# Gate and up products of the experts over 512 columns, and the next expert's transposes placed after the down products

## The chip, the cores and the metric

The kernel runs on one core of a Trainium2 chip. The metric is the time of one execution on the device in microseconds; the figure of the kernel before is the median of its runs, and a profiled execution stands beside them.

## What is computed

The kernel is one layer of an encoder: two token mixers over 2048 tokens of 1024 channels, then a mixture of 16 experts. The change touches the experts alone. Each expert takes the 256 tokens that score highest for it, and adds its weighted output to them:

```python
cap = CAPACITY_FACTOR * T // N_EXPERTS          # 256
top_vals, top_idx = lax.top_k(jnp.swapaxes(affinity, 1, 2), cap)
xs = h[b_idx, top_idx]
hid = jax.nn.silu(jnp.einsum('becd,edf->becf', xs, w_gate)) * jnp.einsum('becd,edf->becf', xs, w_up)
ys = jnp.einsum('becf,efd->becd', hid, w_down) * top_vals[..., None].astype(h.dtype)
return jnp.zeros_like(h).at[b_idx, top_idx].add(ys)
```

## The kernel before, in words

Every number goes into TensorE as two parts of type float32r: a high part (a copy that rounds) and a low part (what the rounding left). A product of two matrices is then three products on TensorE, written in `mm3` (L89 to L93): high weights by high tokens, high weights by low tokens, low weights by high tokens, all into one sum in PSUM. `split` (L96) makes the two parts: a copy on ScalarE (L97) and a subtraction on VectorE (L98).

`stage4` (L1192) walks through 128 parts, n = 0 to 127: 16 experts (e) by 8 blocks (f) of 128 hidden channels. For part n the loop writes, in this order: the splitting of the weights of part n+1 (`weights`, L1256: gate and up together as `wg`, down as `wd`), the load of the raw weights of part n+3 (1.5 MB, on SyncE's queue), the gate and up products of part n (L1330 to L1334: gate, then up, each 8 inner blocks by three products of 256 columns, both into one PSUM tile `pg`), SiLU of the gate on ScalarE (L1336), its product with up on VectorE (L1337), the split of the result into `hd` (L1339), and then the down products of part n-1 (`down`, L1263: 12 products of 512 columns into the four PSUM tiles `py`). So a part is 48 products of 256 columns and 12 of 512 on TensorE.

Beside this, for the next expert: at f = 1 `slots` (L1210) finds the token numbers with 32 small products and issues two gathers of tokens on GpSimd's queue; at f = 3 and f = 4 `turn` (L1241) turns each gathered block `x` of 128 tokens into the layout `xs` of the products. It does so in two halves: four transposes on TensorE into a PSUM tile `pt4`, a copy to the high part on ScalarE (L1248), a subtraction to the low part on VectorE (L1249). The first expert's tokens are turned ahead of the loop (L1315). At f = 0 of the next expert, `result` (L1269) adds the finished `py` tiles to the rows of the output.

The eight PSUM banks of this stage: two for `pt4` (shared by `slots` and `turn`), two for `pg`, four for `py`.

The order in which each engine gets its instructions isn't the order of the text alone. A planner walks through the program with a simulated clock and gives each engine the earliest instruction in the text that is ready by that clock. The order is then fixed, and each engine works it off in turn. `tc.issue_after(ins)` makes the planner place a block's instructions for that engine behind `ins`.

Of the kernel before, what the change touches and what calls it, by code (L numbers as in the profile page):

```python
# [9 lines left out]
F32 = mybir.dt.float32  # L10
F32R = mybir.dt.float32r
BF16 = mybir.dt.bfloat16
I32 = mybir.dt.int32
AF = mybir.ActivationFunctionType
ALU = mybir.AluOpType
AX = mybir.AxisListType
PSUM = bass.MemoryType.PSUM
# [3 lines left out]
KD = D // 128  # L21
# [12 lines left out]
CAP = 2 * T // NEXP  # L34
# [26 lines left out]
def pool(tc, **kw):  # L61

    return tc.tile_pool(reuse_waits="tile", **kw)
# [25 lines left out]
def mm3(nc, out, w, x, start=True, stop=True):  # L89

    nc.tensor.matmul(out, lhsT=w[0], rhs=x[0], start=start, stop=False)  # L91
    nc.tensor.matmul(out, lhsT=w[0], rhs=x[1], start=False, stop=False)  # L92
    return nc.tensor.matmul(out, lhsT=w[1], rhs=x[0], start=False, stop=stop)  # L93


def split(nc, hi, lo, x, eng=None):  # L96
    nc.scalar.activation(hi, x, AF.Copy)  # L97
    (eng or nc.vector).tensor_sub(lo, x, hi)  # L98
# [1093 lines left out]
def stage4(k, out):  # L1192


    nc, tc = k.nc, k.tc
    with ExitStack() as es:
# [4 lines left out]
        xt = es.enter_context(pool(tc, name="xtp", bufs=2))  # L1201
        wr = es.enter_context(pool(tc, name="wr4", bufs=3))
        ws = es.enter_context(pool(tc, name="ws4", bufs=3))
        hp = es.enter_context(pool(tc, name="hp", bufs=2))
# [5 lines left out]
        def slots(e):  # L1210

            ps = ps_t.tile([128, 2, 5], F32, name="pt4")
            for t in range(NBLK):
                o = oh.tile([128, CAP], BF16, name="o")
                nc.vector.tensor_scalar(o, k.iota, k.pos[:, t, e:e + 1], None, op0=ALU.is_equal)
                for h in range(2):
                    nc.tensor.matmul(ps[:, h], lhsT=o[:, h * 128:h * 128 + 128], rhs=k.r5[:, t, e],
                                     start=(t == 0 and h == 0), stop=(t == NBLK - 1), skip_group_check=True)
            g = ip.tile([128, 2, 5], F32, name="g")
            nc.vector.tensor_copy(g, ps)  # L1220
            idx = ip.tile([128, 2], I32, name="idx")
            nc.vector.scalar_tensor_tensor(out=idx, in0=g[:, :, 0], scalar=128.0, in1=g[:, :, 1],
                                           op0=ALU.mult, op1=ALU.add)
            tv = ip.tile([128, 2], F32, name="tv")
            nc.vector.tensor_add(tv, g[:, :, 2], g[:, :, 3])
            nc.vector.tensor_add(tv, tv, g[:, :, 4])
            x = []
            for h in range(2):
                x.append(xg.tile([128, D], F32, name="x"))
                gather(x[h], k.h2, idx[:, h:h + 1])  # L1230
            return idx, tv, x

        def gather(dst, src, idx):
            nc.gpsimd.indirect_dma_start(out=dst, out_offset=None, in_=src,
                                         in_offset=bass.IndirectOffsetOnAxis(ap=idx, axis=0))
# [2 lines left out]
            nc.gpsimd.indirect_dma_start(out=dst, out_offset=bass.IndirectOffsetOnAxis(ap=idx, axis=0),  # L1238
                                         in_=src, in_offset=None)

        def turn(x, xs, h):  # L1241

            for half in range(2):
                pt = ps_t.tile([128, 4, 128], F32, name="pt4")
                for i in range(4):
                    nc.tensor.transpose(pt[:, i], x[h][:, (half * 4 + i) * 128:(half * 4 + i + 1) * 128], k.ident)
                sl = (slice(None), slice(half * 4, half * 4 + 4), slice(h * 128, h * 128 + 128))
                nc.scalar.activation(xs[:, 0][sl], pt, AF.Copy)  # L1248
                nc.vector.tensor_sub(xs[:, 1][sl], pt, xs[:, 0][sl])  # L1249

        def load(n):
            raw = wr.tile([128, 3, KD, 128], F32, name="raw")
            nc.sync.dma_start(raw, k.I["w_exp"][n // KD, n % KD])
            return raw

        def weights(raw, eng=None):  # L1256
            wg = ws.tile([128, 2, 2, KD, 128], F32R, name="wg")
            split(nc, wg[:, 0], wg[:, 1], raw[:, 0:2], eng)
            wd = ws.tile([128, 2, KD * 128], F32R, name="wd")
            split(nc, wd[:, 0], wd[:, 1], raw[:, 2].rearrange("p a b -> p (a b)"), eng)  # L1260
            return wg, wd

        def down(e, f, hd, wd, py):  # L1263
            for h in range(2):
                for n in range(2):
                    mm3(nc, py[h * 2 + n], [hd[:, s, h * 128:h * 128 + 128] for s in range(2)],
                        [wd[:, s, n * 512:n * 512 + 512] for s in range(2)], start=(f == 0), stop=(f == KD - 1))

        def result(py, idx, tv, z, last):  # L1269
            for h in range(2):  # L1270
                ss = fp.tile([128, 1], F32, name="ssf")
                for n in range(2):
                    sl = slice(n * 512, n * 512 + 512)
                    nc.vector.scalar_tensor_tensor(out=z[h][:, sl], in0=py[h * 2 + n], scalar=tv[:, h:h + 1],
                                                   in1=z[h][:, sl], op0=ALU.mult, op1=ALU.add)
                if not last:
                    scatter(k.x2, z[h], idx[:, h:h + 1])
                o = yp.tile([128, D], F32, name="o")
                nc.scalar.activation(o, z[h], AF.Square, accum_out=ss)
                nc.vector.tensor_scalar(ss, ss, 1.0 / D, EPS, op0=ALU.mult, op1=ALU.add)  # L1280
                rs = fp.tile([128, 1], F32, name="rsf")
                rsqrt(k, fp, rs, ss)
                nc.vector.scalar_tensor_tensor(out=o, in0=z[h], scalar=rs, in1=gf, op0=ALU.mult, op1=ALU.mult)
                scatter(out, o, idx[:, h:h + 1])
# [22 lines left out]
        raws = [load(i) for i in range(3, 6)]  # L1307
        small = pieces([x for t in lo for x in t])
        route(k, rp, small)
        ps_t = es.enter_context(pool(tc, name="ps_t4", bufs=2, space=PSUM))  # L1310
        ps_g = es.enter_context(pool(tc, name="ps_g", bufs=2, space=PSUM))
        ps_y = es.enter_context(pool(tc, name="ps_y4", bufs=4, space=PSUM))
        nxt = slots(0)
        xs_n = xt.tile([128, 2, KD, CAP], F32R, name="xs")
        for h in range(2):  # L1315
            turn(nxt[2], xs_n, h)
# [3 lines left out]
        for n in range(N + 1):  # L1320
            e, f = divmod(n, KD)
            if n < N:
                if f == 0:
                    (idx, tv, _), xs = nxt, xs_n
                if 2 < n + 1 < N:
                    w.append(weights(raws.pop(0)))
                if 5 < n + 3 < N:
                    raws.append(load(n + 3))
                wg, wd = w.pop(0)
                pg = ps_g.tile([128, 2, CAP], F32, name="pg")  # L1330
                for a in range(2):
                    for i in range(KD):
                        mm3(nc, pg[:, a], [wg[:, s, a, i] for s in range(2)], [xs[:, s, i] for s in range(2)],
                            start=(i == 0), stop=(i == KD - 1))  # L1334
                sg = hp.tile([128, CAP], F32, name="sg")
                nc.scalar.activation(sg, pg[:, 0], AF.Silu)  # L1336
                nc.vector.tensor_mul(sg, pg[:, 1], sg)  # L1337
                hd = hp.tile([128, 2, CAP], F32R, name="hd")
                split(nc, hd[:, 0], hd[:, 1], sg)  # L1339
            if prev is not None:  # L1340
                pe, pf, phd, pwd, ppy, pidx, ptv = prev
                down(pe, pf, phd, pwd, ppy)
                if pf == KD - 1:
                    result(ppy, pidx, ptv, z, pe + 1 == NEXP)
            if n == N:
                break
            if f == 0:
                py = [ps_y.tile([128, 512], F32, name="py") for _ in range(4)]
            prev = (e, f, hd, wd, py, idx, tv)
            if e + 1 < NEXP:  # L1350
                if f == 1:
                    nxt = slots(e + 1)
                elif f == 3:
                    xs_n = xt.tile([128, 2, KD, CAP], F32R, name="xs")
                    turn(nxt[2], xs_n, 0)
                elif f == 4:
                    turn(nxt[2], xs_n, 1)
            if f == 5:
                z = [yp.tile([128, D], F32, name="z") for _ in range(2)]
                for h in range(2):  # L1360
                    gather(z[h], k.x2, idx[:, h:h + 1])
# [37 lines left out]
def build(tc, I, out, stop=None, mk=None):  # L1399
    k = K()  # L1400
    k.tc, k.nc, k.I, k.stop = tc, tc.nc, I, stop
    with ExitStack() as es:
# [30 lines left out]
        if stop == "stage3":  # L1433
            return
        stage4(k, out)


# [105 lines left out]
```

## Time and profile before

| | us |
|---|---|
| median of 3 runs | 3432.81 |
| lowest, highest | 3432.05, 3434.65 |
| the profiled execution's own time | 3430.81 |
| its span, first to last instruction | 3429.0 |
| stage 4's products, first to last | 2275.4 to 3413.8 of the span |

The times are of the device. The rows in the section below come from the profiled execution; their times are microseconds from its span's start, and L91 is line 91 of the kernel. "PEld" is the load of weights into TensorE, which runs beside a product. A product's row has a modelled end that overlaps the next one's start, so the pace is read from start to start.

### The profile page before, as it was taken

Reading aid. Unit: us, or ns where it says so; the run is one execution under the profiler, and the core shown is the slowest. Engines: PE = TensorE matmul, PEld = TensorE weight load, DVE = VectorE, ACT = ScalarE, POOL = GpSimd, SP = SyncE. Lnnn points to the kernel's source line nnn. Section 1 sums busy time; section 2 is a strip of 40 time slices with the busy share of each in tenths; the row PEclk is TensorE's granted clock in tenths of the full one; section 3 lists DMA queues with packets and bytes.
Section 4 is the critical chain, followed back from the end, with each engine's and each line's share of the span. In section 5 each row is a group of like instructions: output and inputs, shape, how many; then the busy total and the mean of one; then the engine's idle time right before and its main releaser. Section 6 shows DMA issues by size and latency. Waiting matters only on the chain. (4 is left out here: it accounts for less than half of the span.)

```text
span 3429.0 us, 65646 instructions
## 1 busy us (share of the span) xinstructions
PE 3175.8 (93%) x26062; PEld 2609.1 (76%) x26062; DVE 2321.8 (68%) x4902; ACT 1469.0 (43%) x2828; POOL 286.5 (8%) x457
## 2 busy tenths in 40 slices
PE   7999898889879988999979999769999999999998
PEld 6888777667656655666647888559999999999997
DVE  6434679798868889666776666466666666666665
ACT  5111455545434545455553333314444444444443
POOL 0000000000021111001000000001112111121111
PEclk9999999899989998999989999879999999999999
DMA  4222687878787777577656554336666666666663
GB/s 146 83 74 89 186 251 218 244 209 244 217 205 186 166 186 171 141 195 177 178 180 229 197 197 166 147 122 241 218 237 237 245 243 225 230 245 244 236 233 124
DMA packets 464579, 665.19 MB, mean 194 GB/s; under 512 B 162312, under 2 KB 345480, under 8 KB 445968
## 3 DMA queue, kind: packets, MB, share of 16 engines
q1 hardware_dynamic: 387824, 535.14, 50.5%
q10 hardware_dynamic: 58304, 59.79, 5.4%
q0 software_dynamic: 18144, 66.07, 5.1%
q8 instruction: 206, 3.38, 0.4%
q14 instruction: 101, 0.83, 0.1%
HBM read 483.66 MB, written 177.21 MB: 193 GB/s over the span
## 5 line engine op out<-in xcount | busy, mean ns | idle before, releaser
L500 PE MATMUL mm<-h,w 128*128 128x512 f32 x2112 | 604.6, 420 | 26.9 <-ACT ev L524 7.7
L91 PE MATMUL pg<-xs,wg 128*128 128x256 f32 x2048 | 583.7, 285 | 0.0
L92 PE MATMUL pg<-xs,wg 128*128 128x256 f32 x2048 | 582.1, 284 | 0.0
L93 PE MATMUL pg<-xs,wg 128*128 128x256 f32 x2048 | 579.6, 283 | 0.0
L500 PEld LDWEIGHTS mm<-h,w 128*128 128x128 f32 x2112 | 385.7, 195 | 121.2 <-DVE h L98 10.2
L92 PEld LDWEIGHTS pg<-xs,wg 128*128 128x128 f32 x2048 | 392.5, 192 | 4.6 <-DVE xs L1249 0.2
L91 PEld LDWEIGHTS pg<-xs,wg 128*128 128x128 f32 x2048 | 392.3, 192 | 4.6 <-ACT xs L1248 0.2
L93 PEld LDWEIGHTS pg<-xs,wg 128*128 128x128 f32 x2048 | 392.4, 192 | 0.0
L98 DVE TENSOR_TENSOR wg<-raw,wg 128x2048 fp32r<-128x2048 f32 x125 | 286.2, 2290 | 106.0 <-ACT wg L97 105.8
L97 ACT ACTIVATE w<-wraw 128x1024 fp32r<-128x1024 f32 x135 | 142.6, 1058 | 302.5 <-issue 155.1
L1336 ACT ACTIVATE sg<-pg 128x256 f32<-128x256 f32 x128 | 49.3, 385 | 488.2 <-PE pg L93 459.8
L97 ACT ACTIVATE wg<-raw 128x2048 fp32r<-128x2048 f32 x125 | 238.5, 1908 | 0.0
L410 DVE TENSOR_TENSOR tmp<-X,N 128x1 f32<-128x1 f32 (+30 forms) x248 | 188.7, 761 | 40.4 <-DMA N<-pra 26.9
L83 PE MATMUL mm<-h,w 128*128 128x512 f32 x480 | 190.0, 396 | 20.5 <-ACT w L97 12.8
L92 PE MATMUL py<-wd,hd 128*128 128x512 f32 x512 | 203.1, 397 | 0.0
L671 ACT ACTIVATE W<-ps 32x128 f32<-32x128 f32 x512 | 137.1, 268 | 150.0 <-PE ps L666 128.6
L91 PE MATMUL py<-wd,hd 128*128 128x512 f32 x512 | 201.0, 393 | 0.0
L93 PE MATMUL py<-wd,hd 128*128 128x512 f32 x512 | 198.4, 390 | 0.0
L98 DVE TENSOR_TENSOR w<-wraw,w 128x1024 fp32r<-128x1024 f32 x135 | 164.9, 1223 | 47.6 <-ACT w L97 47.2
L84 PE MATMUL mm<-h,w 128*128 128x512 f32 x480 | 188.8, 394 | 0.0
L85 PE MATMUL mm<-h,w 128*128 128x512 f32 x480 | 188.6, 393 | 0.0
L1337 DVE TENSOR_TENSOR sg<-pg,sg 128x256 f32<-128x256 f32 x128 | 54.1, 423 | 192.9 <-ACT sg L1336 192.9
(302 smaller groups left out, 6385.9 us busy)
## 6 DMA issues: line engine op xcount, KB each, us to landing
raw<-w_exp SPq DMA_DIRECT2D x128, 1536.0 KB, 7.7
wraw<-w_in SPq DMA_DIRECT2D x103, 512.0 KB, 4.3
PRA<-pra SPq DMA_DIRECT2D x64, 512.0 KB, 4.7
pra<-PR SPq DMA_DIRECT2D x64, 256.0 KB, 4.3
pra<-A SPq DMA_DIRECT2D x64, 256.0 KB, 3.9
kt<-KT ACTq DMA_DIRECT2D x128, 128.0 KB, 5.0
gl<-ev ACTq DMA_DIRECT2D x64, 256.0 KB, 4.0
KT<-kt SPq DMA_DIRECT2D x128, 128.0 KB, 4.6
```

The lines of the kernel that those rows point to most:

```text
L83: nc.tensor.matmul(ps, lhsT=w[:, 0, i], rhs=hs[i][:, 0], start=(i == 0), stop=False)
L84: nc.tensor.matmul(ps, lhsT=w[:, 0, i], rhs=hs[i][:, 1], start=False, stop=False)
L85: nc.tensor.matmul(ps, lhsT=w[:, 1, i], rhs=hs[i][:, 0], start=False, stop=(i == KD - 1))
L91: nc.tensor.matmul(out, lhsT=w[0], rhs=x[0], start=start, stop=False)
L92: nc.tensor.matmul(out, lhsT=w[0], rhs=x[1], start=False, stop=False)
L93: return nc.tensor.matmul(out, lhsT=w[1], rhs=x[0], start=False, stop=stop)
L97: nc.scalar.activation(hi, x, AF.Copy)
L98: (eng or nc.vector).tensor_sub(lo, x, hi)
L410: nc.vector.tensor_mul(tmp[:, :i, :i], X[:, r, r], col[:, None, :].to_broadcast([128, i, i]))
L500: nc.tensor.matmul(self.ps, lhsT=w[:, t // 2, i], rhs=h[:, t % 2], start=(self.i == 0), stop=(self.i == 3 * KD - 1))
L671: nc.scalar.activation(W[qd(u), o, e].rearrange("p g i -> p (g i)"), ps[qd(u), 128:256], AF.Copy)
L1337: nc.vector.tensor_mul(sg, pg[:, 1], sg)
```

## The change

`mm3` is no longer used for gate and up. Its first two products, which have the same weights, become one product of 512 columns: the high weights by both parts of the tokens (`xs[:, :, i]`, two runs of 256), with the high part's sum in the first 256 columns of a PSUM tile and the low part's in the last 256. The third product, low weights by high tokens, goes on into the first 256 columns. So gate and up each fill a PSUM tile of their own, and the two halves of it are added afterwards: ScalarE copies one half out, VectorE adds the other. `ps_g` has three banks in place of two, and `ps_t` one in place of two.

The next expert's transposes come as one half in each of the parts f = 4, 5, 6 and 7, placed behind the last down product that the same part issues.

```diff
-        def turn(x, xs, h):
+        def turn(x, xs, h, halves=(0, 1)):
-            for half in range(2):
+            for half in halves:
                 pt = ps_t.tile([128, 4, 128], F32, name="pt4")
...
         def down(e, f, hd, wd, py):
             for h in range(2):
                 for n in range(2):
-                    mm3(nc, py[h * 2 + n], [hd[:, s, h * 128:h * 128 + 128] for s in range(2)],
+                    mm = mm3(nc, py[h * 2 + n], [hd[:, s, h * 128:h * 128 + 128] for s in range(2)],
                         [wd[:, s, n * 512:n * 512 + 512] for s in range(2)], start=(f == 0), stop=(f == KD - 1))
+            return mm.ins
...
-        ps_t = es.enter_context(pool(tc, name="ps_t4", bufs=2, space=PSUM))
-        ps_g = es.enter_context(pool(tc, name="ps_g", bufs=2, space=PSUM))
+        ps_t = es.enter_context(pool(tc, name="ps_t4", bufs=1, space=PSUM))
+        ps_g = es.enter_context(pool(tc, name="ps_g", bufs=3, space=PSUM))
...
-                pg = ps_g.tile([128, 2, CAP], F32, name="pg")
+                gu = []
                 for a in range(2):
+                    pg = ps_g.tile([128, 2, CAP], F32, name="pg")
                     for i in range(KD):
-                        mm3(nc, pg[:, a], [wg[:, s, a, i] for s in range(2)], [xs[:, s, i] for s in range(2)],
-                            start=(i == 0), stop=(i == KD - 1))
-                sg = hp.tile([128, CAP], F32, name="sg")
-                nc.scalar.activation(sg, pg[:, 0], AF.Silu)
-                nc.vector.tensor_mul(sg, pg[:, 1], sg)
+                        nc.tensor.matmul(pg, lhsT=wg[:, 0, a, i], rhs=xs[:, :, i], start=(i == 0), stop=False)
+                        nc.tensor.matmul(pg[:, 0], lhsT=wg[:, 1, a, i], rhs=xs[:, 0, i], start=False,
+                                         stop=(i == KD - 1))
+                    t = hp.tile([128, CAP], F32, name=f"gu{a}")
+                    nc.scalar.activation(t, pg[:, 1], AF.Copy)
+                    nc.vector.tensor_add(t, pg[:, 0], t)
+                    gu.append(t)
+                    if a == 0:
+                        nc.scalar.activation(t, t, AF.Silu)
+                sg = gu[0]
+                nc.vector.tensor_mul(sg, gu[1], sg)
...
-                down(pe, pf, phd, pwd, ppy)
+                last = down(pe, pf, phd, pwd, ppy)
...
-                elif f == 3:
-                    xs_n = xt.tile([128, 2, KD, CAP], F32R, name="xs")
-                    turn(nxt[2], xs_n, 0)
-                elif f == 4:
-                    turn(nxt[2], xs_n, 1)
+                elif f >= 4:
+                    if f == 4:
+                        xs_n = xt.tile([128, 2, KD, CAP], F32R, name="xs")
+                    with tc.issue_after(last):
+                        turn(nxt[2], xs_n, (f - 4) // 2, (f % 2,))
```

## Rows read from the trace of the kernel before

**Rows 1.** The page's first part: busy time, share of the span, instructions.

```profile
PE 3175.8 (93%) x26062; PEld 2609.1 (76%) x26062; DVE 2321.8 (68%) x4902; ACT 1469.0 (43%) x2828; POOL 286.5 (8%) x457
```

**Rows 2.** Windows: one stretch, its length, busy time of each engine, clock, DMA.

```profile
2400.00:3400.00 1000.00, 1000.00 (x7405) 936.57 (x7404) 650.34 (x1209) 456.07 (x561) 162.37 (x110) 1.00 0.64 232
```

**Rows 3.** Timeline of PE, one part: start, length, engine, line, operation, tiles.

```profile
2700.13 0.40 PE L91 MATMUL py<-wd,hd 128*128 128x512 f32 x1
2700.36 0.40 PE L92 MATMUL py<-wd,hd 128*128 128x512 f32 x1
2700.60 0.39 PE L93 MATMUL py<-wd,hd 128*128 128x512 f32 x1
...
2702.88 0.28 PE L91 MATMUL pg<-xs,wg 128*128 128x256 f32 x1
2702.99 0.28 PE L92 MATMUL pg<-xs,wg 128*128 128x256 f32 x1
...
2703.35 0.28 PE L92 MATMUL pg<-xs,wg 128*128 128x256 f32 x1
...
2708.63 0.40 PE L91 MATMUL py<-wd,hd 128*128 128x512 f32 x1
```

**Rows 4.** Timeline of ACT over the end of a part, idle time and releaser in brackets.

```profile
2407.30 0.39 ACT L1336 ACTIVATE sg<-pg 128x256 f32<-128x256 f32 x1 [4.08 <-PE pg L93]
2407.58 1.91 ACT L97 ACTIVATE wg<-raw 128x2048 fp32r<-128x2048 f32 x1
2409.38 0.40 ACT L97 ACTIVATE hd<-sg 128x256 fp32r<-128x256 f32 x1
2409.99 1.06 ACT L97 ACTIVATE wd<-raw 128x1024 fp32r<-128x1024 f32 x1 [0.20 <-PE py L93]
```

**Rows 5.** Timeline of DVE over the same stretch.

```profile
2407.72 0.42 DVE L1337 TENSOR_TENSOR sg<-pg,sg 128x256 f32<-128x256 f32 x1 [2.58 <-ACT sg L1336]
2409.52 2.29 DVE L98 TENSOR_TENSOR wg<-raw,wg 128x2048 fp32r<-128x2048 f32 x1 [1.38 <-ACT wg L97]
2411.73 0.42 DVE L98 TENSOR_TENSOR hd<-sg,hd 128x256 fp32r<-128x256 f32 x1
2412.06 1.22 DVE L98 TENSOR_TENSOR wd<-raw,wd 128x1024 fp32r<-128x1024 f32 x1
```

**Rows 6.** Timeline of all engines where one block of tokens is turned.

```profile
2396.22 1.04 PE L1246 MATMUL pt<-ident,x 128*128 128x128 f32 x8
2396.86 1.09 ACT L1248 ACTIVATE xs<-pt 128x512 fp32r<-128x512 f32 x2 [4.53 <-PE pt L1246]
...
2397.02 0.36 PE L92 MATMUL pg<-xs,wg 128*128 128x256 f32 x1
...
2397.22 0.28 PE L93 MATMUL pg<-xs,wg 128*128 128x256 f32 x1
```

**Rows 7.** Timeline of all engines ahead of the first part.

```profile
2271.08 1.97 PE L1246 MATMUL pt<-ident,x 128*128 128x128 f32 x8 [5.86 <-DMA x<-h,idx]
2272.23 0.60 ACT L1248 ACTIVATE xs<-pt 128x512 fp32r<-128x512 f32 x1 [43.74 <-PE pt L1246]
2272.86 0.69 DVE L1249 TENSOR_TENSOR xs<-pt,xs 128x512 fp32r<-128x512 f32 x1 [6.90 <-ACT xs L1248]
...
2273.61 1.97 PE L1246 MATMUL pt<-ident,x 128*128 128x128 f32 x8 [0.56 <-DVE xs L1249]
...
2275.41 0.79 PE L91 MATMUL pg<-xs,wg 128*128 128x256 f32 x2
```

**Rows 8.** Timeline of PE in the first expert, at f = 3 and f = 4.

```profile
2315.61 1.07 PE L1246 MATMUL pt<-ident,x 128*128 128x128 f32 x8 [0.62 <-DMA x<-h,idx]
...
2321.98 1.06 PE L1246 MATMUL pt<-ident,x 128*128 128x128 f32 x8 [0.89 <-DMA x<-h,idx]
```

**Rows 9.** Timeline of all engines in the last part.

```profile
3409.80 0.42 DVE L98 TENSOR_TENSOR hd<-sg,hd 128x256 fp32r<-128x256 f32 x1 [0.48 <-ACT hd L97]
...
3410.96 0.39 PE L91 MATMUL py<-wd,hd 128*128 128x512 f32 x1
```

## The prediction

> **What bounds the kernel now.** I read the page's busy times first: TensorE (PE) is busy 93% of the span, VectorE (DVE) 68%, ScalarE (ACT) 43% [rows 1]. That is a mean over several stages, so the second view is the windows of the stage that the change touches. From 2400 to 3400 us PE is busy for 1000 of 1000 us at a granted clock of 1.00 (2.4 GHz), while DVE is at 65%, ACT at 46% and the DMA engines at 64% [rows 2]. So in the expert loop PE is the only bound, and only two things count: what PE's instructions take, and whether PE is made to wait. But a PE that is "busy" may hide pauses, as the rows' ends overlap; the third view, PE's timeline of one part from start to start, settles that. The 48 gate and up products of 256 columns go from 2702.88 to 2708.63, which is 119.8 ns each, and the 12 down products of 512 columns from 2700.13 to 2702.88, 229 ns each [rows 3]. A part takes 8.50 us without a hole.
>
> The two paces tell where the gain can lie. At 2.4 GHz 256 columns stream in 106.7 ns and 512 in 213.3; the rows show 120 and 229. Each product thus costs some 13 to 16 ns over its columns, whatever its length. Fewer, longer products save that start cost.
>
> **The change, part by part.**
>
> *The products.* An inner index takes three products of 256 now, 3 x 119.8 = 359.4 ns [rows 3]. After it takes one of 512 and one of 256, with the same 768 columns and one start fewer. No stretch of the trace alternates the two lengths, but the seams of a part show both neighbourhoods. A 512 product straight behind a 256 one takes 230 ns (2700.13 to 2700.36), the next 240, and the mean of the twelve is 229; the first 256 product behind a 512 one takes 110 (2702.88 to 2702.99), and the first four take 470 together, 117.5 each [rows 3]. I take 229 + 117.5 = 346.7 ns, the middle of what stands beside a seam: 12.7 ns saved. There are 128 parts x 2 x 8 = 2048 such pairs, so **-26.0 us**. The ends: 229 + 110 = 339 ns saves 20 ns a pair, 41 us; 240 + 120 = 360 ns saves nothing.
>
> Here the Trainium skill speaks against the change: "TensorE: Matmul & The Clock Gate", section "Back-to-back issue gap", gives the gap of isolated products as columns over clock plus 2.5 ns. By that one start less would be worth 5 us in all. The trace doesn't agree: 120 ns for 256 columns is 13 ns over the stream, not 2.5, and this is what the sum uses.
>
> *The second run of the tokens.* The moving operand of the 512 product is two runs of 256. The trace has no such product to compare with. If the second run cost as much as a new product, the 512 would take 240 ns, the same end of zero gain as above; if it costs nothing, the sum stands. I take nothing, as the pace in rows 3 follows columns and starts, and keep the end.
>
> *The evacuation.* Before, a part has one SiLU (0.39 us, ACT) and one product (0.42, DVE) that read PSUM [rows 4, 5]. After, it has two ACT copies, a SiLU, two DVE additions and the product: by the same rows +0.78 us on ACT and +0.84 on DVE for each part. DVE's share goes to some 75%, ACT's to 55%. What hides it is the down product's place: `hd` of a part is needed only behind the next part's gate and up. The low half of `hd` starts at 2411.73, 4.4 us after the SiLU at 2407.30, and the down products that need it start 8.2 us after that SiLU [rows 4, 5]. A delay of 0.85 us fits in the 3.4 us left. The gate's half moves forward besides, as it no longer shares a PSUM tile with up. With three `pg` banks a bank is written again three groups later, over 5 us. So nothing, though 0.84 us on each of 128 parts, 108 us, if that slack weren't there.
>
> *The transposes in the loop.* Eight cost PE 0.80 us, and the product behind them takes 0.20 in place of 0.12 [rows 6]: 0.11 us each, in batches of four as of eight. Each half moves with its four transposes, its ACT copy and its DVE subtraction; no DMA is issued by it, so SP and POOL see nothing of the move. In number and length they stay: 0.
>
> *The first expert.* At its f = 3 and f = 4 PE waited 0.62 and 0.89 us for the gathers [rows 8]. One part or more later these have landed: **-1.5 us**, and at worst nothing.
>
> *Ahead of the loop.* All four halves of the first tokens now go through one bank, so each waits for the subtraction of the one before. The rows show this step once, as the third half waited so with two banks: 2271.08 to 2273.61, 2.53 us [rows 7]. The fourth then starts at 2271.08 + 3 x 2.53 = 2278.67, takes half of the 1.97 us that eight take here, and the first gate product comes at 2279.65 in place of 2275.41: **+4.2 us**; +3.3 if the planner puts that product ahead of the last transposes.
>
> *The added wait.* The last half of the next expert's tokens is now turned at the very end of f = 7, and the next gate needs it from inner index 4 on, both high and low. Lay this on rows 4 to 6. Transposes from 2409.80, their result 0.64 us later (2410.44). ACT is in the copy of `wd`, which waits for the same down products, until 2411.05; the copy of the half then ends at 2411.65. DVE has the low half of `wg` and `hd` until 2412.15, then the subtraction, 0.69 us: 2412.84. PE, after 0.44 us of transposes and four inner indices of 0.347 us, wants it at 2411.63. That is a wait of 1.2 us, or 2.4 if the low half of `wd` (1.22 us) goes first. What covers it: the first four inner indices of up, 1.39 us, need nothing of that half. The planner takes what is ready by its clock, and rows 6 show that it breaks into a triple of products (the eight transposes stand between an L91 and its L92). With up put there the wait is 0 to 1.0 us. I take 0.3 at each of 15 boundaries, **+4.5 us**; the ends are 0 and 2.4, which is 36 us.
>
> *The tail.* In the last part `hd` is ready at 3410.22, and its down products start at 3410.96 behind those of the part before [rows 9]. The evacuation is longer by one addition, 0.45 us: hidden, 0.
>
> *Sum.* -26.0 - 1.5 + 4.2 + 4.5 = -18.8 us, against the profiled execution's own 3430.8: 3412.0. The median of the runs is 2.0 above that execution, so 3414 for the median.
>
> **The rivals.**
>
> *The expert's first gate waits (17%).* One place, f = 7 to f = 0; the price b is set by whether the planner's clock has the half ready sooner than the chip does, in which case nothing stands in the hole. For it: the planner was early twice in rows 8. Against: those were gathers, not engine work. The rest of the sum is -23.3 us, so the change loses once 15 b is above that, b over 1.55 us, and loses measurably over 2.0 us. At b = 1.2 the time is 3414 - 4.5 + 18 = 3427.5; at 2.4 it is 3445.5, slower than before. I give 8% to slower and 9% to the stretch in between.
>
> *The pair costs 360 ns (8%).* Either two runs cost as two products, or the excess over the stream goes with columns rather than starts. Then the gain is gone and the time is 3414 + 26 = 3440, just on the edge of slower. Against it: 256 columns carry nearly the same excess as 512 [rows 3]. The gap of the Trainium skill cited above, from "TensorE: Matmul & The Clock Gate", would end close by, at 3435 with its 5 us of gain.
>
> *The pair costs 339 ns and up covers every boundary (10%).* Then -41 - 1.5 + 4.2 = -38.3, 3394.5. For it: the 110 ns step.
>
> **How the numbers follow.** The forecast has 65%, with its own range of 3403 to 3424 (pairs of 343 to 350 ns, boundaries of 0 to 0.8 us). The range of 8 in 10 takes in the upper half of the big gain and most of the boundary rival: 3401 to 3432. A measurement of this kernel can tell about 0.2%, 6.9 us, from no change. Faster by more: the forecast and the big gain, 0.75. Within it: the milder boundary wait and half of the 360 ns, 0.14. Slower: the long boundary wait and the rest, 0.11.
>
> **What would show it.** On PE's timeline, steps of about 0.23 and 0.12 us in turn inside a part, a part of some 8.3 us, and a stage still without holes. On the waits, PE or its weight load behind the `xs` subtraction 15 times, with the length of each. Ahead of the loop, the first gate product 4 us later; no wait for a gather in the first expert. DVE at about 75% in the windows. I am wrong if the 512 product takes 240 ns or more, if the boundary waits sum to over 20 us, or if PE waits for `hd`, `wg` or a `pg` bank in the parts f = 0 to 2, where DVE also has the results and the slots to do.

## The result, and the profile after

| | before | after |
|---|---|---|
| median of 4 runs, us | 3433.73 | 3494.95 |
| lowest, highest | 3432.05, 3435.47 | 3490.06, 3499.12 |
| the profiled execution's own time | 3430.81 | 3490.06 |
| its span | 3429.0 | 3488.3 |

The ratio is 1.0178 (95% interval 1.0163 to 1.0194): slower, where 3414 and faster were forecast, and far outside the range. The first view after is the page's busy line; it answers to [rows 1].

```profile
PE 3187.7 (91%) x24014; PEld 2504.9 (72%) x24014; DVE 2409.0 (69%) x5158; ACT 1559.7 (45%) x3084; POOL 304.8 (9%) x457
```

PE has 2048 products fewer and its share has fallen. The windows of the stage say that it pauses now (stretch, its length, busy time and count of PE, PEld, DVE, ACT, POOL, granted clock, DMA share, GB/s); the first line answers to [rows 2].

```profile
2400.00:3400.00 1000.00, 956.76 (x5288) 797.97 (x5288) 687.04 (x1362) 507.89 (x743) 169.61 (x104) 0.97 0.61 222
...
2400.00:2600.00 200.00, 199.96 (x1138) 167.14 (x1138) 146.76 (x297) 108.52 (x159) 32.35 (x22) 1.00 0.64 238
2600.00:2800.00 200.00, 186.55 (x1010) 155.34 (x1009) 132.99 (x248) 98.73 (x145) 32.88 (x19) 0.97 0.58 213
```

1000 busy us of 1000 have become 957, and the granted clock 1.00 has become 0.97. Up to 2600 us nothing of that is to be seen. The waits from 2285 to 3480 us name it (what waited, for what; us in total, times, longest; `x` is the tile that a gather fills):

```profile
PE pt L1246 <- DMA x<-h,idx: 43.0, 9, 5.4
...
PEld pt L1246 <- DVE xs L1249: 6.2, 14, 0.5
```

The transposes wait for the gathered tokens `x`, at 9 of 15 experts. The wait that was forecast as the danger, of the next expert's gate for the last half's subtraction, is not in the list. The second line is another one, 14 times and small: the last half's transposes wait for the one `pt4` bank, until the third half's subtraction (L1249) is done. PE's timeline at the first of the nine:

```profile
2611.89 0.39 PE L91 MATMUL py<-wd,hd 128*128 128x512 f32 x1
2616.43 0.66 PE L1246 MATMUL pt<-ident,x 128*128 128x128 f32 x4 [4.16 <-DMA x<-h,idx]
...
2619.51 0.63 PE L1335 MATMUL pg<-xs,wg 128*128 128x512 f32 x1
...
2620.15 0.63 PE L1335 MATMUL pg<-xs,wg 128*128 128x512 f32 x1
...
2620.79 0.39 PE L1335 MATMUL pg<-xs,wg 128*128 128x512 f32 x1
...
2621.14 0.40 PE L1335 MATMUL pg<-xs,wg 128*128 128x512 f32 x1
```

From the start at 2611.89 to the next at 2616.43 pass 4.54 us. The pause also costs something after it: a pair of products takes 640 ns from 2619.51 to 2620.15, and 350 ns from 2620.79 to 2621.14. The windows around it show the clock:

```profile
2611.90:2616.40 4.50, 0.38 (x2) 0.00 (x0) 2.05 (x2) 0.00 (x0) 0.00 (x0) 1.00 0.84 340
2616.90:2620.80 3.90, 3.90 (x16) 3.34 (x15) 1.92 (x2) 1.55 (x2) 0.00 (x0) 0.56 0.01 2
2620.80:2625.00 4.20, 4.20 (x26) 3.65 (x26) 1.20 (x3) 2.03 (x4) 0.00 (x0) 1.00 0.95 348
```

Behind the idle stretch PE works at a granted clock of 0.56, near the lower level of 1.2 GHz, until 2620.8.

**The account.** Steps are taken from a product's start to the next one's. Over the nine pauses they are 46.5 us, 44.4 more than nine usual steps of 0.23. In the 9 us behind each of them PE's work takes 1.4 to 2.9 us more than at its usual paces, 20.9 in all. So the waits cost 65.3 us, by which the stage from the first gate product to the last down product would be longer; it is 55.6 longer (1193.7 against 1138.1). All the rest of the change is thus worth -9.7 us there, and the first gate product comes 3.6 us later.

**Why the tokens are late.** Three things come before the first of the nine waits. First, the index of the tokens, `idx`, is late. PE's last small product of `slots` (L1217), ACT's copy and DVE's subtraction for the weights of a later part stand like this:

```profile
2596.68 0.20 PE L1217 MATMUL pt<-r,o 128*128 128x5 bf16 x2
...
2597.26 1.92 ACT L97 ACTIVATE wg<-raw 128x2048 fp32r<-128x2048 f32 x1 [3.17 <-DMA raw<-w_exp]
...
2599.21 2.29 DVE L98 TENSOR_TENSOR wg<-raw,wg 128x2048 fp32r<-128x2048 f32 x1 [4.67 <-ACT wg L97]
```

That subtraction stands ahead of `idx` in DVE's queue. DVE is idle for 4.67 us in front of it, because ACT waits for a load of raw weights. SP could issue this load only at 2588.28, 19 us behind the one ahead of it, as its buffer came free with a subtraction of `wd` that ends at 2588.25; in the kernel before, the loads of this stretch are 7 to 10 us apart. So `idx` starts 6.3 us behind the end of PE's last small product, and 5.6 to 6.9 at the nine experts; before it was 0.3. That is more than any of the nine waits, but no run changes this delay alone.

Second, the gather's issue is held, and third, a load goes out ahead of it meanwhile. DVE's timeline of after, where `idx` is made, then the gathers of POOL (GpSimd) and the loads of SP (SyncE; the two loads are issued at 2602.94 and about 2607.5):

```profile
2603.16 0.15 DVE L1222 SCALAR_TENSOR_TENSOR idx<-g 128x2 int32<-128x2 f32 x1
...
2603.70 2.28 DVE L98 TENSOR_TENSOR wg<-raw,wg 128x2048 fp32r<-128x2048 f32 x1
2605.91 0.42 DVE L1345 TENSOR_TENSOR gu<-gu,gu 128x256 f32<-128x256 f32 x1
2606.24 1.22 DVE L98 TENSOR_TENSOR wd<-raw,wd 128x1024 fp32r<-128x1024 f32 x1
2607.38 0.42 DVE L98 TENSOR_TENSOR hd<-gu,hd 128x256 fp32r<-128x256 f32 x1
```

```profile
2604.05 4.58 POOL L1234 DMA_INDIRECT x<-h,idx  x1 [16.40 <-PE py L93]
2608.93 0.94 POOL L1234 DMA_INDIRECT x<-h,idx  x1 [0.30 <-issue]
...
2602.94 4.88 SPq L1253 DMA_DIRECT2D raw<-w_exp  x2
```

The gather's issue on POOL takes 4.58 us here, 3.6 more than the usual 0.95; this is called the hold below. It ends at 2608.63, 0.83 us behind the end of DVE's run at 2607.80; `wg`, `gu`, `wd` and `hd` of that run all read two tiles in SBUF. By then a 1.5 MB load of weights has been issued, at about 2607.5. At all nine experts the gather lands 0.2 to 1.0 us behind that load. The summaries of single gathers, of before at 2602.0 and of after at 2604.1 and 2460.7, show what follows (duration in ns, start; the landing, when the data have arrived, from the issue's start in us):

```profile
L1234 POOL DMA_INDIRECT x<-h,idx x1: 946/946/946, 2602.0 to 2602.0; - x1
...
DMA to landing us min/median/max: 5.2/5.2/5.2
```

```profile
L1234 POOL DMA_INDIRECT x<-h,idx x1: 4577/4577/4577, 2604.1 to 2604.1; - x1
...
DMA to landing us min/median/max: 12.3/12.3/12.3
...
L1234 POOL DMA_INDIRECT x<-h,idx x1: 964/964/964, 2460.7 to 2460.7; - x1
...
DMA to landing us min/median/max: 6.3/6.3/6.3
```

Before, from the second expert on, the transposes came 7.5 to 7.7 us after the gather's start, and the gather landed 5.2 to 6.5 us after it. After, at the nine experts with an issue of 4.57 or 4.58 us, PE gets to them at about the same distance (2611.89 is 7.84 us behind 2604.05; the nine lie between 7.2 and 8.4) and the tokens land at 12.3 to 13.5. At the other experts the issue takes 0.96 to 2.9 us, the landing 6.0 to 9.0, and nothing waits.

### The profile page after: what moved, and what is told of

It is laid out like the page before. It is cut to its first block, busy times and chain, and to the rows that moved or that the text cites. A ratio compares the mean times of both kernels' runs of the same rounds, so it can differ in the third digit from the quotient of the medians.

```text
span 3488.3 us, 61985 instructions
## 1 busy us (share of the span) xinstructions
PE 3187.7 (91%) x24014; PEld 2504.9 (72%) x24014; DVE 2409.0 (69%) x5158; ACT 1559.7 (45%) x3084; POOL 304.8 (9%) x457
## 5 line engine op out<-in xcount | busy, mean ns | idle before, releaser
L1335 PE MATMUL pg<-xs,wg 128*128 128x512 f32 x2048 | 745.7, 404 | 0.0
L1336 PE MATMUL pg<-xs,wg 128*128 128x256 f32 x2048 | 584.2, 285 | 0.0
L1335 PEld LDWEIGHTS pg<-xs,wg 128*128 128x128 f32 x2048 | 392.6, 192 | 90.3
L1336 PEld LDWEIGHTS pg<-xs,wg 128*128 128x128 f32 x2048 | 395.0, 193 | 5.1
L1339 ACT ACTIVATE gu<-pg 128x256 f32<-128x256 f32 x256 | 97.0, 380 | 251.4 <-PE pg L1336 217.9
L1340 DVE TENSOR_TENSOR gu<-pg,gu 128x256 f32<-128x256 f32 x256 | 106.5, 421 | 149.1 <-ACT gu L1339 149.0
L92 PE MATMUL py<-wd,hd 128*128 128x512 f32 x512 | 205.4, 401 | 0.0
L91 PE MATMUL py<-wd,hd 128*128 128x512 f32 x512 | 204.7, 400 | 0.0
L93 PE MATMUL py<-wd,hd 128*128 128x512 f32 x512 | 177.7, 400 | 0.0
L97 ACT ACTIVATE wd<-raw 128x1024 fp32r<-128x1024 f32 x125 | 132.1, 1057 | 89.7 <-PE py L93 89.4
L98 DVE TENSOR_TENSOR wd<-raw,wd 128x1024 fp32r<-128x1024 f32 x125 | 152.6, 1221 | 24.0 <-ACT wd L97 24.0
```

The lines of the kernel that those rows point to most:

```text
L1335: nc.tensor.matmul(pg, lhsT=wg[:, 0, a, i], rhs=xs[:, :, i], start=(i == 0), stop=False)
L1336: nc.tensor.matmul(pg[:, 0], lhsT=wg[:, 1, a, i], rhs=xs[:, 0, i], start=False, stop=(i == KD - 1))
```

## The experiments

The theory: the waits come from the two parts together, since the added DVE work delays and holds the gathers, and the moved transposes are placed where the planner's clock has the tokens landed. The rivals: the products alone, the move alone, DVE's load in general, the hold alone without the loads.

**1. The products alone.** The changed kernel with the transposes and banks as before.

```diff
-                elif f >= 4:
...
-                    with tc.issue_after(last):
-                        turn(nxt[2], xs_n, (f - 4) // 2, (f % 2,))
+                elif f == 3:
...
+                    turn(nxt[2], xs_n, 0)
+                elif f == 4:
+                    turn(nxt[2], xs_n, 1)
```

> The merged products and their evacuation alone; the transposes stay at f = 3 and 4 with two banks, and gate and up have two banks. Theory G (the time went to PE waiting for the gathered tokens at the moved transposes): pairs of 351 ns against 359 give 18 us, no wait at a transpose over 1 us, time about 3416. Rival D (the added work on DVE and ACT is what makes the gathers late, wherever the transposes stand): waits of 4 to 6 us at most experts as in the changed kernel, time 3470 or more.

3421.8 us, ratio 0.9972 (0.9960 to 0.9984). No wait for `x` in the loop, and 1000 of 1000 us busy from 2400 to 3400. DVE does all the added work here, yet `idx` comes 1.2 us behind the last small product, in front of a pause of DVE, and the gathers are issued in 0.94 to 0.96 us. The products alone gain.

**2. The move alone.** The moved transposes with one `ps_t` bank, gate and up as before.

```diff
...
-                        nc.tensor.matmul(pg, lhsT=wg[:, 0, a, i], rhs=xs[:, :, i], start=(i == 0), stop=False)
...
+                        mm3(nc, pg[:, a], [wg[:, s, a, i] for s in range(2)], [xs[:, s, i] for s in range(2)],
...
```

> The moved transposes with one bank alone; products and evacuation as before. Theory G with the place as the cause: waits of about 5 us at most experts, each with some 2 us of low clock behind it, time 3480 to 3500. Rival D (the added DVE work makes the gathers late): no wait for a gather, only the serial start with one bank, time 3434 to 3440.

3433.94 us, ratio 1.0006 (0.9995 to 1.0018). Gathers are issued in 0.95 us and nothing in the loop waits for them. So neither part brings the waits by itself.

**3. The gathers one part earlier.**

```diff
-                if f == 1:
+                if f == 0:
                     nxt = slots(e + 1)
```

> The changed kernel with the slots and gathers of the next expert written at f = 0 in place of f = 1, some 8 us earlier. Theory G: the tokens have landed when PE comes to the transposes, no wait over 1 us, the 51 us of waits and some 20 us of low clock are gone, time 3420 to 3430. Rival B (the single bank or the last half at the expert's end costs the time): 3480 or more.

3429.36 us, ratio 0.9990 (0.9981 to 1.0000). PE's waits for `x` fall from 43.0 us to 4.1, at 3 places. The tokens were the cause. The run takes the hold away too (each expert's first gather is issued in 0.96 us from 2380 us on), so it doesn't part hold and place; and landings of 8.7 to 10.4 us, 13.3 at the last expert, with two loads in flight, leave little of the part won.

**4. The low part of `wg` in four pieces** of 0.7 us each in place of one of 2.3.

```diff
-            split(nc, wg[:, 0], wg[:, 1], raw[:, 0:2], eng)
+            nc.scalar.activation(wg[:, 0], raw[:, 0:2], AF.Copy)
+            for a in range(2):
+                for j in range(0, KD, 4):
+                    nc.vector.tensor_sub(wg[:, 1, a, j:j + 4], raw[:, a, j:j + 4], wg[:, 0, a, j:j + 4])
```

> The changed kernel with the low part of gate and up weights subtracted in four pieces of 512 columns in place of one of 2048 on DVE. Theory G with the gather blocked by long DVE instructions: the first gather's issue on POOL falls from 4.58 us to under 2.5, the waits shrink by 2 to 4 us at 9 experts, time 3460 to 3477. Rival (the issue's 4.58 us has another cause): it stays at 4.6, time 3490 to 3505 with the added fixed cost of the pieces.

3422.02 us, ratio 0.9966 (0.9954 to 0.9979); every gather in the loop from 2450 us on is issued in 0.94 to 0.96 us. That looked like proof that the seams let the gather through. Run 10 shows that it isn't: here DVE was idle for 3.35 us right behind `idx`.

**5 and 6. The hold by itself.** The kernel before, with two added DVE instructions of 128x2048 behind `tv`, whose results nothing reads: in 5 a subtraction with two inputs in SBUF, in 6 a maximum over one.

```diff
...
+            with tc.issue_after(done.ins):
+              for _ in range(2 if e else 0):
+                nc.vector.tensor_sub(dm, dm, dm)
```

```diff
...
+            with tc.issue_after(done.ins):
+              for _ in range(2 if e else 0):
+                nc.vector.tensor_reduce(out=dr, in_=dm, op=ALU.max, axis=AX.X)
```

> The kernel before with two subtractions of 128x2048 on DVE (two inputs from SBUF, results unused) right behind tv at each expert from the second on; every other instruction keeps its place. Theory G with the gather blocked by DVE: the first gather's issue on POOL goes from 0.95 us to between 3 and 8, the transposes of f = 3 wait 2 to 8 us at 14 or 15 experts, time 3465 to 3560. Rival Q (the gather was late from the DMA queues and the raw loads alone): the issue stays at 0.95, no wait, time 3428 to 3437.

> The same with two reductions of 128x2048 to 128x1 (one input from SBUF) in the same places, about the same time on DVE. If only DVE instructions with two inputs from SBUF block the gather: its issue stays near 0.95 us or takes at most the 2.3 us of the weights' subtraction behind the dummies, waits under 1 us, time 3428 to 3440. If any busy DVE blocks it, or if it is the late DVE itself that costs the time: as with the two-input dummies, 3465 or more.

POOL's and DVE's timeline at one expert, in 5 and then in 6:

```profile
2611.78 2.53 POOL L1239 DMA_INDIRECT x<-h,idx  x1 [11.31 <-PE pg L93]
...
2611.20 2.29 DVE L1231 TENSOR_TENSOR dm<-dm 128x2048 f32<-128x2048 f32 x1
```

```profile
2601.49 0.95 POOL L1240 DMA_INDIRECT x<-h,idx  x1 [12.73 <-PE pg L93]
...
2600.91 2.28 DVE L1232 TENSOR_REDUCE dr<-dm 128x1 f32<-128x2048 f32 x1
```

As long a DVE instruction holds the gather with two SBUF inputs (2.53 us in place of 0.95) and does not with one. The Trainium skill has this rule: in "SBUF — State Buffer", section "Who interferes with whom", "A DVE instruction with two SBUF inputs contends with a GpSimd instruction that reads SBUF". These two runs agree with it; the issue, which takes its rows from `idx` in SBUF, ends 0.82 us behind the first subtraction's end at 2613.49. The two dummies also differ in what they write, 2048 columns against one. Two gathers beside instructions of one size settle that: of the changed kernel beside an addition of a PSUM and an SBUF tile, and of run 9 beside a product of two SBUF tiles.

```profile
3153.57 0.42 DVE L1340 TENSOR_TENSOR gu<-pg,gu 128x256 f32<-128x256 f32 x1 [0.76 <-ACT gu L1339]
3153.62 0.93 POOL L1234 DMA_INDIRECT x<-h,idx  x1 [0.30 <-issue]
```

```profile
3312.85 0.43 DVE L1345 TENSOR_TENSOR gu<-gu,gu 128x256 f32<-128x256 f32 x1
3312.91 1.18 POOL L1234 DMA_INDIRECT x<-h,idx  x1 [0.30 <-issue]
```

Both write 256 columns; only the one with two SBUF inputs holds the issue, until 0.81 us behind its end. In all the traces, 31 issues of gathers and scatters that begin beside such an addition take 0.93 to 0.98 us; of eleven beside such a product ten take 1.17 to 1.21 and one 1.00. Neither kernel of runs 5 and 6 is slower (ratios 0.9999, 0.9990 to 1.0009, and 1.0003, 0.9990 to 1.0015). In 5 the held gather lands at 6.8 us, before the transposes. A hold of 1.6 us does nothing while that margin stands.

**7. Pieces and earlier gathers together.** The edits of 3 and 4.

> The changed kernel with the low part in four pieces and the slots at f = 0. Theory G: the gather leaves in 0.95 us and has a part more to land, no wait at a transpose over 0.5 us, time 3412 to 3420. Rival (the rest of the missing gain is the single bank, not waits for tokens): no better than with the pieces alone, 3421 to 3425.

A miss: 3441.12 us, ratio 1.0017 (1.0005 to 1.0028). The issue takes about 1.3 us, but each expert's first gather lands at 11.8 to 17 us from 2380 us on, and PE waits 16.0 us for `x` at 7 experts. A gather that isn't held is late too where two loads are in flight. The theory needed its second half: what else the DMA engines carry.

**8. Products of one length together,** on run 1's kernel.

```diff
                         nc.tensor.matmul(pg, lhsT=wg[:, 0, a, i], rhs=xs[:, :, i], start=(i == 0), stop=False)
+                    for i in range(KD):
                         nc.tensor.matmul(pg[:, 0], lhsT=wg[:, 1, a, i], rhs=xs[:, 0, i], start=False,
...
```

> The products-only kernel with the eight products of 512 columns of gate or up first and the eight of 256 behind them, so that the lengths change twice per group in place of sixteen times. If the change of length is what makes the pair 352 ns in place of the forecast 347: pairs of 346 to 348, time 8 to 12 us less than products only, 3410 to 3414. If not: pairs of 351 to 353 and the same time within 4 us.

3410.75 us, ratio 0.9930 (0.9912 to 0.9947): the best kernel of the study. PE's timeline of one part, from start to start:

```profile
2703.87 1.98 PE L1335 MATMUL pg<-xs,wg 128*128 128x512 f32 x8
2705.69 1.12 PE L1337 MATMUL pg<-xs,wg 128*128 128x256 f32 x8
2706.64 2.00 PE L1335 MATMUL pg<-xs,wg 128*128 128x512 f32 x8
2708.48 1.11 PE L1337 MATMUL pg<-xs,wg 128*128 128x256 f32 x8
2709.43 0.40 PE L91 MATMUL py<-wd,hd 128*128 128x512 f32 x1
```

Sixteen pairs take 5.56 us (2703.87 to 2709.43), 347.5 ns each. Over the loop the median steps here are 227 and 120 ns, 347 a pair; in turn they are 236 and 117 in run 1 and 233 and 117 in the changed kernel, 353 and 350.

**9. The transposes one part later:** halves in f = 5, 6, 7 and 7.

```diff
-                elif f >= 4:
-                    if f == 4:
+                elif f >= 5:
+                    if f == 5:
...
-                        turn(nxt[2], xs_n, (f - 4) // 2, (f % 2,))
+                        turn(nxt[2], xs_n, 0 if f < 7 else 1, (f - 5,) if f < 7 else (0, 1))
```

> The changed kernel with its halves one part later: the first in f = 5, the second in f = 6, the third and fourth both in f = 7. DVE's order around idx and the gathers' issue stay as in the changed kernel. Theory (the gathers are late, by their issue behind DVE's two-input work and by landing beside the next weights, and the transposes of f = 4 come at them 4.5 to 5.7 us too early): a part of 8.3 us is more than every such wait, so the waits for x at the transposes go to under 5 us in all, the granted clock of the loop returns to 1.00 in every 200 us, and the gathers' issues are still about 4.6 us at many experts. Both halves in f = 7 may add up to 2 us at each of 15 boundaries. Time 3415 to 3445. Rival (PE is held up by DVE's added work as such, and the wait for x only stands where PE happens to show it): the waits move to another place of the part and the time stays at 3480 or above.

3430.48 us, ratio 0.9998 (0.9986 to 1.0009); no wait for `x` in the loop, clock 1.00 in every 200 us. But the expected holds are missing: the planner put a pause of DVE behind `idx`, and every issue but the first expert's takes 0.94 to 1.2 us. So the run doesn't show that a later place alone would do. It does price two halves in one part: PE waits 8.1 us for L1249 in all, 15 times.

**10 and 11. The changed kernel with the four pieces and one length together (10), and the changed kernel once more (11).** Run 10 has the edits of 4 and 8.

> The changed kernel with the low part of wg in four subtractions of 512 columns and, in each gate or up group, the eight products of 512 first, then the eight of 256. Theory: issues of the gathers at 0.96 us and few waits for x as in the run with pieces alone (3422), and a pair at 347.7 ns in place of 350.7, 2048 x 3 ns = 6 us less: 3412 to 3419. Against the run with long products first and the transposes left at f = 3 and f = 4 (3410.75) it tells what the move of the transposes is worth: by this theory nothing or a few us lost; by the rival (the spread transposes take pauses out of PE, once the tokens are there in time) it comes out under 3405.

> The changed kernel with one edit that leaves the rest of it as it is: the eight products of 512 of a gate or up group first, then the eight of 256. Theory: the pair goes from 350.7 to 347.7 ns, 6 us less in all, but the waits for x at the transposes of f = 4 stay (some 45 to 55 us and the low clock behind them): 3475 to 3495. Rival (the waits hang on the products' order, or on a chance of one execution): the waits are under 20 us and the time under 3450.

The edit that run 11's expectation names is not in the kernel that ran: it is the changed kernel line for line, and its products of 512 and 256 columns still come in turn. So it says nothing on the products' order. As a second run of the changed kernel it shows that the waits are no chance of one execution: 3498.47 us, ratio 1.0215 (1.0171 to 1.0258), PE waits 48.8 us for `x`, at 11 experts. Run 10 is a clear miss: 3501.77 us, ratio 1.0211 (1.0193 to 1.0229), waits of 51.8 us at 11. DVE's and POOL's timeline of run 10, then of run 4:

```profile
2615.75 0.15 DVE L1222 SCALAR_TENSOR_TENSOR idx<-g 128x2 int32<-128x2 f32 x1
...
2616.30 2.49 DVE L1261 TENSOR_TENSOR wg<-raw,wg 128x512 fp32r<-128x512 f32 x4
...
2620.18 0.42 DVE L98 TENSOR_TENSOR hd<-gu,hd 128x256 fp32r<-128x256 f32 x1
...
2616.65 4.79 POOL L1234 DMA_INDIRECT x<-h,idx  x1 [17.07 <-PE py L93]
```

```profile
2602.66 0.15 DVE L1222 SCALAR_TENSOR_TENSOR idx<-g 128x2 int32<-128x2 f32 x1
...
2606.24 1.90 DVE L1261 TENSOR_TENSOR wg<-raw,wg 128x512 fp32r<-128x512 f32 x3 [3.35 <-ACT wg L1258]
...
2603.56 0.96 POOL L1234 DMA_INDIRECT x<-h,idx  x1 [7.94 <-issue]
```

Four short subtractions in a row hold the gather as one long one does: its issue ends at 2621.44, 0.84 us behind `hd`. What saved run 4 is where `idx` fell, in front of a pause of DVE and 0.3 us behind PE's last small product; the same pieces with another order of the products put it in front of a run, 5.0 to 7.6 us behind.

**12. The load of f = 1 written in f = 2.**

```diff
-                if 5 < n + 3 < N:
+                if 5 < n + 3 < N and f != 1:
+                    if f == 2 and 5 < n + 2:
+                        raws.append(load(n + 2))
                     raws.append(load(n + 3))
```

> The changed kernel with the raw weights that it loads in f = 1 loaded in f = 2 instead, ahead of that part's own load, so that no 1.5 MB load sits beside the gathers of f = 1; DVE's work and the transposes' places are the changed kernel's. Theory (two things add up: the gather's descriptors are held up behind DVE's run of two-input work, and then the load, which came first, is served first): the gathers' issues are still about 4.6 us at many experts, they land 6 to 9 us after their start in place of 12.3 to 13.5, the transposes wait 0 to 1.5 us each in place of 4.5 to 5.7, and the time is 3415 to 3445. Rival one (the held issue alone makes the wait): the waits stay above 4 us and the time at 3480 or more. Rival two (the two loads in f = 2 are late for the splitting of their weights): no wait for x, but ACT's split of wg waits for raw in f = 4 and PE behind it, and the time is above 3450.

3494.24 us, ratio 1.0210 (1.0172 to 1.0249), nothing told apart: SP still issues a load 3.4 us behind each held gather. The wrong one was moved. SP's loads go out in the order of their parts, and the one behind the changed kernel's gather at 2604.05 is the load of part 41, which the loop writes at f = 6. Within the run, three first gathers with issues of 0.96 us land at 6.4 to 6.6 us; eight held for 4.58 at 12.4 to 13.5, and the transposes wait for all of these.

**13. Without the load of f = 7's weights,** which the loop writes at f = 4. The kernel leaves that load out and uses the weights of f = 6 twice, so it does not compute the layer.

```diff
-                    raws.append(load(n + 3))
+                    raws.append(load(n + 3) if f != 4 else raws[-1])
```

> The changed kernel without the load that part f = 4 issues, the one that starts 3.4 us behind the held gathers: the weights of f = 7 are those of f = 6 again, read from the same tile. Theory (hold and load add up): where a gather's issue is held to 4.58 us it lands 8 to 10 us after its start (5.4 plus the hold of 3.6, at most) in place of 12.3 to 13.5, and the transposes wait 0 to 2 us each in place of 4.5 to 5.7; the time is under 3450. Rival one (the hold alone): landings of held gathers stay above 11.5 us, waits above 4 us, and the time above 3475. Rival two (the load alone): held gathers land at 5.4 to 7 us, as if they had not been held.

3428.7 us, ratio 0.9986 (0.9972 to 1.0000). The load that is left out is not the one behind the gathers, as its expectation has it (that is f = 6's, as in run 12); but with one load fewer each later one gets its buffer sooner. Around the held gather at 2606.90 a load starts 1.1 us ahead, as in the changed kernel, and the next only 11.7 us behind, where the changed kernel has one 3.4 us behind. A gather's summary, and PE's timeline at its transposes:

```profile
L1234 POOL DMA_INDIRECT x<-h,idx x1: 4574/4574/4574, 2606.9 to 2606.9; - x1
...
DMA to landing us min/median/max: 8.2/8.2/8.2
```

```profile
2614.55 0.39 PE L91 MATMUL py<-wd,hd 128*128 128x512 f32 x1
2615.10 0.66 PE L1246 MATMUL pt<-ident,x 128*128 128x128 f32 x4 [0.17 <-DMA x<-h,idx]
```

Twelve gathers are held for 4.57 to 4.59 us as before, and land at 7.7 to 8.2. PE waits 1.6 us for `x` in the whole loop, and its clock is 1.00 in every 200 us. So a hold of 3.6 us makes a gather some 2.7 us late against 5.2; the load ahead of it adds the other 4 to 6. The changed kernel's pause needs both: held past the load's issue, the gather lands behind the load. The late index is there in this run too (5.2 to 7.1 us behind the last small product) and costs hardly a wait there. A leaner DMA load for the whole stage, 16 loads of 128 fewer, is part of this run; it did not shorten the hold, since the gathers are held as long as before and only their landings moved.

## Why the prediction was wrong, point by point

- **The evacuation, "So nothing".** This is the step that failed. It weighed DVE's added work against the slack of `hd` alone, and put everything else at nothing. In place of that nothing the runs show 65.3 us, the waits for the tokens and the low clock behind them. The slack of `hd` was there: no product waits for `pg`, `wg` or `hd` by more than 0.3 us. But what else stands in DVE's queue, and what POOL and PE then wait for, was not asked. At the nine experts `idx` stands behind a subtraction that waits for its weights, and in front of a closed run of two-input work, to which the product of gate and up now belongs (it reads two SBUF tiles, where L1337 read PSUM); so the index is 6 us late and the gather is held for 3.6. The added work alone does not bring this order (run 1), nor does the move (run 2): the sum priced two parts one by one that act on one chain. Which of DVE's instructions tips the order was not separated.
- **The transposes, "SP and POOL see nothing of the move".** The move issues nothing there, true; but at the nine experts it leaves PE at the transposes 7.2 to 8.4 us behind a gather that now needs 12.3 to 13.5: as near as before, though they are placed later, because the index comes later too. Rows 8 had shown that the planner takes tokens for landed too early. I read them as a price of 1.5 us, to be saved; they were the warning. The 1.5 us were saved.
- **The products, -26.0 us.** The mechanism was right and the size off by a quarter: the pair measures 350 ns against 346.7 taken, 2048 x 9.4 = -19.3 us. By steps from start to start, run 13's gate and up products take 727.3 us against 746.4 before, -19.1. The 229 and 117.5 of the seam rows come from products that mostly stand beside their own kind; in turn the 512 takes 233. With each length together, in run 8, they give 720.5 us, -25.9: the forecast's own term, but by an order of the products that it did not have. The bet against the issue gap of the Trainium skill ("TensorE: Matmul & The Clock Gate", section "Back-to-back issue gap") held: the 5 us estimated by it were too few.
- **The down products, not in the sum.** Run 13's take 367.0 us against 354.6, and 2.0 of that are its own waits. So some 10 us are lost where nothing was forecast. The boundary (below) is 2.5 of it. Another 3.6 are the down products behind a batch of transposes: 42 of them now, which take 0.315 us in place of 0.229; before, a gate or up product stood there each time. The rest, some 4 us, I did not follow.
- **Ahead of the loop, +4.2 us.** Right: from the first transposes to the first gate product it took 4.33 us [rows 7]; PE's timeline after gives 8.33, +4.0, in steps of 2.53 us as taken:

```profile
2270.68 1.09 PE L1246 MATMUL pt<-ident,x 128*128 128x128 f32 x4 [6.05 <-DMA x<-h,idx]
2273.19 1.11 PE L1246 MATMUL pt<-ident,x 128*128 128x128 f32 x4 [1.41 <-DVE xs L1249]
...
2279.01 0.78 PE L1335 MATMUL pg<-xs,wg 128*128 128x512 f32 x1
```

- **The boundary, 0.3 us each.** Near in size, by luck: the wait that was priced, at the next gate, did not come, and with it the rival with the most weight. What is paid there is another: the last half's transposes wait for the one bank and come about 0.41 us behind the product ahead of them in place of 0.23, 14 x 0.18 = 2.5 us against 4.5.
- **The tail, 0.** Right: from the start of the last down product to the end of the span it is 15.6 us, and 15.5 before.

None of the prediction's signs of being wrong named the wait that came, PE's for the tokens. Without the waits the change would have come out near run 13's 3428.7, some 5 us better than before and still 15 short of the forecast; this is an estimate, as run 13 leaves out loads too.

## What to carry to other kernels

Before adding work to an engine that has time to spare, list what stands in its queue behind it and ends up somewhere else: here an index for a gather, which landed at 5.2 to 6.5 us for transposes at 7.5 to 7.7, a margin of 1.2 to 2.5 us. In these runs a gather issued by POOL was not safe beside a run of DVE instructions with two SBUF inputs; place the index in front of a pause of DVE, and the gather ahead of the next big load. And of two edits that are each harmless alone (runs 1 and 2), ask what margin each takes from the same chain.

## What had not been expected of the hardware

- A gather's issue of 0.95 us stretches to 2.53 us beside a 2.29 us subtraction and to 4.58 or 4.79 beside a run of two-input work, shorter pieces included, while a 2.28 us reduction of one input leaves it at 0.95. Why a hold ends behind a single instruction at some places and only behind the whole run at others stays open; at 3225.61 in the changed kernel a gather that starts 0.03 us behind the start of such a subtraction isn't held at all (0.96 us).
- Held past the issue of a 1.5 MB load, a gather lands at 12.3 to 13.5 us in place of 5.2; held as long without the load, at 7.7 to 8.2.
- Products of 512 and 256 columns in turn cost 350 to 353 ns a pair, eight of each together 347 (runs 1 and 8 and the changed kernel).
- A pause of 4.5 to 5.7 us costs 1.4 to 2.9 us more behind it, at a granted clock of 0.56 (2616.9 to 2620.8 us).
